# One-tensor divisions on GpSimd, and fixed places for w_out's splits in layer 0 of a two-layer encoder

## The chip, the cores and the metric

One core of a Trainium2 chip runs the whole kernel. The engines named below are TensorE (PE; its weight loads are PEld), VectorE (DVE), ScalarE (ACT), GpSimd (POOL) and SyncE (SP), which issues the DMAs here. The metric is the device time of one execution in microseconds (us), the median of several runs.

## The reference

A two-layer encoder over 1024 tokens of width 1024, all in float32. Layer 0 has three groups of attention heads, layer 1 two; both end with a gate and an output projection:

```python
def even_layer(x, mem_n, table, norm_g, w_in, sink, q_norm, k_norm, w_mem_kv, w_out):
    h = rmsnorm(x, norm_g)
    aq, ak, av, bq, bk, bv, xq, gate = _split(h @ w_in, EVEN_SPLITS)
    y_a = windowed_gqa_sink(heads(aq, A_HEADS), heads(ak, A_KV_HEADS), heads(av, A_KV_HEADS), sink, table)
    ...
    y_b = dense_gqa_blocked(qb, kb, heads(bv, B_KV_HEADS))
    y_x = memory_cross_attention(heads(xq, X_HEADS), mem_n, w_mem_kv)
    y = jnp.concatenate([y_a..., y_b..., y_x...], axis=-1) * jax.nn.silu(gate)
    return x + y @ w_out
```

Group A attends within a window of 128 keys on either side (with a sink logit), group B densely over all 1024 keys, group X over 256 memory tokens. Each of these has a softmax, and so a division by a row's sum. The norms divide by a row's root mean square.

## The kernel before

TensorE multiplies in a reduced float32 form. To keep the accuracy, each operand is split in a high half (the value rounded to that form) and a low half (what is left), and a product is made of three matmuls: high by high, high by low, low by high. The weights are split on the chip as they arrive: for w_in by `load_w` (tiles wr, wh, wl; high on VectorE, L239, low mostly on GpSimd, L241), for w_out by `load_wout` (raw tile wor, halves woh and wol). A w_out piece is 128 rows by 512 columns, and a layer has 16. In layer 0, piece i has its high half on ScalarE (L257) and its low half on GpSimd if i is odd, on VectorE if even (L258).

A piece's raw tile comes from two rings that others use too: "wr" with 2 buffers for even i, "sg" with 3 for odd i. A transfer into a raw buffer waits until the low half of the piece before in it has been made.

Layer 0's attention is a list of steps, which `run_steps` works through. A step of group B (wide: one head, 128 queries, 1024 keys) does this: scores on TensorE (sb), a row minimum on VectorE (L1061), a scalar and the exponential on ScalarE (L1065, L1066; the tile e, and its sum z), the reciprocal rz of the sum on VectorE (L1069) and the division of e by it on GpSimd (L1070). A step of group A (narrow) handles two blocks of 128 queries with at most 384 keys each (L1140, L1144, L1148, and two divisions at L1154). The steps come in the pattern B B A. One step later SP copies the divided tile into another (er) by DMA, which only renames its type. Three steps after its scores the tile is transposed on TensorE (te for B at L540, ta for A at L1175) into a PSUM tile, of which there are two, and split in halves: PTh on ScalarE (L315), PTl on VectorE (L316). Every second step the values are multiplied in (ob at L1083, oa at L1192). The result is joined on ScalarE and VectorE (yt, L437 and L438) and gated on GpSimd (gy, L439).

Between these, projections (acc, L297) are pulled in to fill TensorE, and late in layer 0 parts of the output projection (pre, L662), which need w_out's halves and chunks of the gated result (raw yr, halves yh on ScalarE and yl on VectorE, L318 and L319). `wout_hook` asks for a w_out piece at most once in each of its calls, which come twice in a step.

At the start of the kernel x and the memory tokens are normed: a sum of squares on ScalarE, a power on GpSimd (L229), and a scaling per row, on VectorE (L336) or, with slow=True, on GpSimd (L335). That is so for the fifth x tile and the two memory tiles (memt), which TensorE transposes next (tm, L979).

Every engine works its queue in order. The order of a queue is not the order of the program's text: a scheduler in the framework places the instructions, and `tc.issue_after(x)` holds what is recorded under it behind the instruction x.

Of the kernel before, what the change touches and what calls it, by code (L numbers as in the profile page):

```python
# [14 lines left out]
AF = mybir.ActivationFunctionType  # L15
ALU = mybir.AluOpType
# [139 lines left out]
def encoder_kernel(ctx, tc, A):  # L156
# [93 lines left out]
    def load_wout(l, i, pl):  # L250
        nh, k = divmod(i, 8)
        if k == 0:
            wtile.append([pl.tile([P, 8, 512], F32R, tag="h", name="wo" + c, bufs=4) for c in "hl"])
        raw = sg(M, "wor", F32) if i % 2 else wp.tile([P, 512], F32, tag="wr", name="wor", bufs=2)
        dma(raw, w_out[l][KORD[l][k], :, nh * 512:(nh + 1) * 512])
        hi, lo = (t[:, k, :] for t in wtile[nh])
        (nc.vector.tensor_copy if WHI[l] else nc.scalar.copy)(hi, raw)  # L257
        (nc.gpsimd if i % 2 else nc.vector).tensor_tensor(out=lo, in0=raw, in1=hi, op=ALU.subtract)  # L258
        return hi, lo

    def wout_hook(l, jobs, last, pl):
# [5 lines left out]
                wout[len(wout)] = load_wout(l, len(wout), pl)  # L267

    wout, wtile, half = {}, [], [0]
    chunks = {}  # L270

    def half_done(n=1):
# [59 lines left out]

    def scale_tile(xt, r, slow=False):
        if slow:
            return nc.gpsimd.tensor_tensor(out=xt, in0=xt, in1=r.to_broadcast([P, D]), op=ALU.mult)  # L335
        return nc.vector.tensor_scalar(out=xt, in0=xt, scalar1=r, scalar2=None, op0=ALU.mult)  # L336

    def transpose_tile(xt, hT, t):
# [697 lines left out]
    if True:  # L1036
        def b_step(h, qb):
            st = Step()
            st.sub = qb % 2
            st.fill = 3 if h == 0 else 1  # L1040
            if st.sub == 0:
                bgrp["g"] = {}
            grp = st.grp = bgrp["g"]
            e = [None]

            def s1(h=h, qb=qb, e=e):
                if qb == 2 and h < 5:
                    jobs.ensure("bq%d" % ((h + 1) // 2))
                    load_q(Bq, bq_d, h + 1)
                if h == NB0 and qb == 0:  # L1050
                    jobs.ensure("bq2")
                    open_ab()
                    jobs.ensure("aq0")
                    load_q(Aq, aq_d, 0)
                    a_bias(0)
                Sp = ps_s("sb")
                for j in range(2):
                    qk(Sp[:, j * 512:(j + 1) * 512], Bq[h], qb * P, B["k"][h // 3], B["kl"][h // 3],
                       j * 512, 512)
                mn = stat("mn")  # L1060
                nc.vector.tensor_reduce(out=mn, in_=Sp, op=ALU.min, axis=AX.X)  # L1061
                et = new_e(M)
                z = stat("z")
                mr = stat("mr")
                nc.scalar.activation(mr, mn, AF.Identity, scale=rq[:, qb, h:h + 1])  # L1065
                nc.scalar.activation(et, Sp, AF.Exp, bias=mr, scale=nrq[:, qb, h:h + 1], accum_out=z)  # L1066
                def finish():
                    rz = stat("rz")
                    nc.vector.reciprocal(rz, z)  # L1069
                    nc.gpsimd.tensor_tensor(out=et, in0=et, in1=rz.to_broadcast([P, 1024]), op=ALU.mult)  # L1070
                    e[0] = et
                return finish
            st.s1 = s1
            st.hop = word_copy(M, e)
            st.s2 = dense_s2(M, e, st)
            if st.sub == 1:
                def s3(h=h, qb=qb, grp=grp):
                    ph, pl_ = grp["pt"]
                    acc = ps_a("ob")[:, :256]
                    n = 0  # L1080
                    for kt in range(8):
                        for pt in (ph, pl_):
                            nc.tensor.matmul(acc, B["v"][:, kt, h // 3, :], pt[:, kt, :],  # L1083
                                             start=(n == 0), stop=(n == 15))
                            n += 1
                    y_evac(M, acc, gates[3 + h // 2], h % 2, (qb - 1) * P)
                    if h % 2 == 1 and qb == 7:
                        store_y(0, KORD[0].index(3 + h // 2), gates[3 + h // 2])
                st.s3 = s3
                st.need3 = ("bv", "g%d" % (3 + h // 2))  # L1090
            st.need = ("bk", "bq%d" % (h // 2))
            return st
# [18 lines left out]
    if True:  # L1111
        def a_step(h, p):
# [5 lines left out]
            def s1(h=h, p=p, e=e):  # L1118
# [15 lines left out]
                for j in range(2):  # L1134
# [6 lines left out]
                                                   in1=abias[h][:, c:c + n], scale=1.0,  # L1141
                                                   scalar=nsink[:, h:h + 1], op0=ALU.add, op1=ALU.min,
                                                   accum_out=mn[:, j:j + 1])
                    nc.scalar.activation(et[:, j, c:c + n + 1], et[:, j, c:c + n + 1], AF.Exp,  # L1144
                                         bias=mn[:, j:j + 1], scale=-1.0, accum_out=z[:, j:j + 1])
                def finish():
                    rz = stat("rz2", 2)
                    nc.vector.reciprocal(rz, z)  # L1148
                    for j in range(2):
# [1 line left out]
                        lo, hi = max(0, qb - 1) * P, min(8, qb + 2) * P  # L1151
                        c = lo - (qb - 1) * P
                        ej = et[:, j, c:c + hi - lo]
                        nc.gpsimd.tensor_tensor(out=ej, in0=ej, in1=rz[:, j:j + 1].to_broadcast([P, hi - lo]), op=ALU.mult)  # L1154
                    e[0] = et
                return finish
            st.s1 = s1
# [55 lines left out]
            wout_hook(0, jobs, "g2", r1)  # L1213

    run_steps(steps, jobs, hooks0, lambda i: i % 4 != 3)
    jobs.drain()
    top_stack.close()
    att.close()
# [377 lines left out]
```

## Time and profile before

| | us |
|---|---|
| median of 3 runs | 1242.44 (1242.15 to 1243.17) |
| the profiled execution | 1241.79 |
| its span, first to last instruction | 1240.0 |

| engine | share of the span busy |
|---|---|
| TensorE, matmuls | 97% |
| TensorE, weight loads | 81% |
| VectorE | 65% |
| ScalarE | 53% |
| GpSimd | 33% |

A row of a group reads: line, engine, operation, output<-inputs, output shape<-input shape, count | busy us, mean ns of one | idle us just before them, and what ended most of that. A row of the timeline has start and length in us first, and in square brackets the idle time before it and the instruction that ended it. A row of the waits has: engine, what waits <- what is waited for: us in all, times, the longest. A row of the stretches is explained where it stands.

### The profile page before, as it was taken

The numbers are of one execution on the slowest core, as the hardware profiler recorded it, in microseconds if no ns is written. First come the engines' busy times: TensorE is split into PE (matmuls) and PEld (weight loads), VectorE is DVE, ScalarE is ACT, GpSimd is POOL, SyncE is SP. The second block draws the span as 40 slices with busy tenths as digits, with TensorE's granted clock in tenths as the row PEclk, the third lists the DMA queues.
The fourth block names the chain that finished last, engine by engine and source line by source line (L and its number), as shares of the span: only waits on it lengthen the run. The fifth ranks groups of instructions, "written<-read, shape, count | busy, mean of one in ns | idle before, by whom it ended". The sixth has DMA issues, their size and how long they took to land. (4 is left out here: it accounts for less than half of the span.)

```text
span 1240.0 us, 19680 instructions
## 1 busy us (share of the span) xinstructions
PE 1202.2 (97%) x6806; PEld 999.9 (81%) x6806; DVE 805.7 (65%) x1479; ACT 651.9 (53%) x1453; POOL 412.1 (33%) x390
## 2 busy tenths in 40 slices
PE   5999999999999899999999999999999999999997
PEld 4788888888887788877888788888787878877886
DVE  5547665477777778647356866766767676678544
ACT  6248754367667776533157633544444454456322
POOL 5023365466666655403022221222222121223100
PEclk9999999999999999999999999999999999999999
DMA  6664445545465565376545333242342432546354
GB/s 255 195 194 146 161 170 167 164 159 202 175 229 203 193 236 198 149 211 224 170 151 162 119 111 123 88 143 102 111 134 79 139 112 102 162 141 203 119 197 147
DMA packets 96638, 199.91 MB, mean 161 GB/s; under 512 B 11510, under 2 KB 31222, under 8 KB 96540
## 3 DMA queue, kind: packets, MB, share of 16 engines
q1 hardware_dynamic: 96540, 198.66, 47.7%
q8 instruction: 54, 0.88, 0.3%
q14 instruction: 44, 0.36, 0.1%
HBM read 79.32 MB, written 31.47 MB: 89 GB/s over the span
## 5 line engine op out<-in xcount | busy, mean ns | idle before, releaser
L297 PE MATMUL acc<-h,wh 128*128 128x512 f32 x1536 | 499.2, 398 | 2.1 <-DVE wh L239 0.8
L297 PEld LDWEIGHTS acc<-h,wh 128*128 128x128 f32 x1536 | 283.1, 188 | 66.9 <-issue 12.4
L297 PE MATMUL acc<-h,wl 128*128 128x512 f32 x768 | 304.5, 396 | 1.0 <-POOL wl L241 1.0
L241 POOL TENSOR_TENSOR wl<-wr,wh 128x512 fp32r<-128x512 f32 x96 | 124.4, 1296 | 334.5 <-DVE wh L239 147.2
L316 DVE TENSOR_TENSOR PTl<-te,PTh 128x512 fp32r<-128x512 f32 x224 | 148.3, 686 | 120.9 <-ACT PTh L315 118.3
L1448 ACT ACTIVATE e<-e,mn 128x1024 f32<-128x1024 f32 x96 | 110.1, 1149 | 126.2 <-DVE mn L1445 126.1
L297 PEld LDWEIGHTS acc<-h,wl 128*128 128x128 f32 x768 | 144.5, 188 | 34.0 <-issue 4.7
L315 ACT CAST PTh<-te 128x512 fp32r<-128x512 f32 x224 | 125.0, 590 | 18.3 <-PE te L540 15.2
L1445 DVE CUSTOM_DVE_ANT_0 e<-sc,toep 128x1024 f32<-128x1024 f32 x96 | 114.0, 1216 | 5.8 <-PE sc L1439 5.6
L1070 POOL TENSOR_TENSOR e<-e,rz 128x1024 f32<-128x1024 f32 x48 | 92.5, 1931 | 74.3 <-DVE rz L1069 56.6
L540 PEld LDWEIGHTS te<-identr,er 128*128 128x128 f32 x896 | 92.2, 143 | 18.1 <-issue 3.2
L540 PE MATMUL te<-identr,er 128*128 128x128 f32 x896 | 99.2, 246 | 5.3 <-issue 2.5
L239 DVE CAST wh<-wr 128x512 fp32r<-128x512 f32 x112 | 56.3, 504 | 42.1 <-PE acc L297 17.8
L1457 DVE SCALAR_TENSOR_TENSOR e<-e,mr 128x1024 f32<-128x1024 f32 x48 | 76.3, 1589 | 1.3
L1472 PE MATMUL oc<-PTh,v 128*128 128x256 f32 x384 | 74.8, 288 | 0.3 <-DVE ckl L1341 0.3
L662 PE MATMUL po<-woh,yl 128*128 128x512 f32 (+1 forms) x172 | 65.6, 382 | 0.0
L662 PE MATMUL po<-woh,yh 128*128 128x512 f32 (+1 forms) x172 | 65.6, 381 | 0.0
L662 PE MATMUL po<-wol,yh 128*128 128x512 f32 (+1 forms) x172 | 65.4, 380 | 0.0
L1061 DVE TENSOR_REDUCE mn<-sb 128x1 f32<-128x1024 f32 x48 | 58.4, 1216 | 7.2 <-PE sb L509 6.8
L1472 PEld LDWEIGHTS oc<-PTh,v 128*128 128x128 f32 x384 | 61.4, 191 | 0.6 <-DVE ckl L1341 0.5
L1066 ACT ACTIVATE e<-sb,mr,nrq 128x1024 f32<-128x1024 f32 x48 | 58.0, 1208 | 1.9
L318 ACT ACTIVATE yh<-yr 128x256 fp32r<-128x256 f32 (+2 forms) x56 | 23.9, 447 | 64.1 <-DMA yr<-ysc 30.2
(199 smaller groups left out, 2248.4 us busy)
## 6 DMA issues: line engine op xcount, KB each, us to landing
er<-e SPq DMA_DIRECT2D x112, 512.0 KB, 3.0
wr<-in_w_in SPq DMA_DIRECT2D x96, 256.0 KB, 2.7
ysc<-gy SPq DMA_DIRECT2D x16, 512.0 KB, 2.6
wor<-in_w_out SPq DMA_DIRECT2D x32, 256.0 KB, 3.4
cq<-sg SPq DMA_DIRECT2D x64, 128.0 KB, 2.5
ck<-sg SPq DMA_DIRECT2D x48, 128.0 KB, 2.3
er<-e SPq DMA_DIRECT2D x12, 384.5 KB, 2.9
xpsc<-xh SPq DMA_DIRECT2D x18, 256.0 KB, 2.4
```

Of the source, the lines that this page charges most:

```text
L241: (nc.vector if fast else nc.gpsimd).tensor_tensor(out=lo, in0=raw, in1=hi, op=ALU.subtract)
L297: lastmm[0] = nc.tensor.matmul(acc, a, b[:, k, c0:c0 + n], start=(i == 0), stop=(i == 23))
L315: nc.scalar.copy(hi, src)
L316: return nc.vector.tensor_tensor(out=lo, in0=src, in1=hi, op=ALU.subtract)
L540: nc.tensor.transpose(to[:, i * P:(i + 1) * P], e[0][:, k * P:(k + 1) * P], idt)
L662: lastmm[0] = nc.tensor.matmul(acc, a, b, start=(start and n == 0), stop=(stop and n == 2))
L1061: nc.vector.tensor_reduce(out=mn, in_=Sp, op=ALU.min, axis=AX.X)
L1070: nc.gpsimd.tensor_tensor(out=et, in0=et, in1=rz.to_broadcast([P, 1024]), op=ALU.mult)
L1445: nc.vector.tensor_tensor_reduce(out=et, in0=Sp, in1=toeps[h][:, w0:w0 + 1024], scale=1.0, scalar=BIG, op0=ALU.add, op1=ALU.min, accum_out ...
L1448: nc.scalar.activation(et, et, AF.Exp, bias=mn[:, m:m + 1], scale=-1.0, accum_out=z[:, m:m + 1])
L1457: nc.vector.scalar_tensor_tensor(out=es[0], in0=es[1], scalar=c, in1=es[0], op0=ALU.mult, op1=ALU.add)
L1472: nc.tensor.matmul(acc, V[:, kt, v, :], pt[:, kt, :], start=(n == 0), stop=(n == 23))
```

## The change

Two things change. First, where GpSimd divides a softmax tile (L1070, L1154) or scales a row (L335), it no longer multiplies two tensors, of which one is a column broadcast along the row; it runs the form with one tensor and a factor per partition. Second, in layer 0 the two halves of a w_out piece are held behind the softmax steps: the high half behind the last exponential recorded before it, the low half behind the last division recorded before it, and all low halves are on GpSimd. `behind` keeps those two instructions; after the steps its entry is cleared. Layer 1's pieces are placed as before.

```diff
--- before.py
+++ after.py
@@ -254,8 +254,11 @@
         raw = sg(M, "wor", F32) if i % 2 else wp.tile([P, 512], F32, tag="wr", name="wor", bufs=2)
         dma(raw, w_out[l][KORD[l][k], :, nh * 512:(nh + 1) * 512])
         hi, lo = (t[:, k, :] for t in wtile[nh])
-        (nc.vector.tensor_copy if WHI[l] else nc.scalar.copy)(hi, raw)
-        (nc.gpsimd if i % 2 else nc.vector).tensor_tensor(out=lo, in0=raw, in1=hi, op=ALU.subtract)
+        own = l == 0 and behind["sub"] is not None
+        with (tc.issue_after(behind["exp"].ins) if own else nullcontext()):
+            (nc.vector.tensor_copy if WHI[l] else nc.scalar.copy)(hi, raw)
+        with (tc.issue_after(behind["sub"].ins) if own else nullcontext()):
+            (nc.gpsimd if own or i % 2 else nc.vector).tensor_tensor(out=lo, in0=raw, in1=hi, op=ALU.subtract)
         return hi, lo
 
     def wout_hook(l, jobs, last, pl):
@@ -267,6 +270,7 @@
                 wout[len(wout)] = load_wout(l, len(wout), pl)
 
     wout, wtile, half = {}, [], [0]
+    behind = {"exp": None, "sub": None}
     chunks = {}
 
     def half_done(n=1):
@@ -332,7 +336,7 @@
 
     def scale_tile(xt, r, slow=False):
         if slow:
-            return nc.gpsimd.tensor_tensor(out=xt, in0=xt, in1=r.to_broadcast([P, D]), op=ALU.mult)
+            return nc.gpsimd.tensor_scalar(out=xt, in0=xt, scalar1=r, scalar2=None, op0=ALU.mult)
         return nc.vector.tensor_scalar(out=xt, in0=xt, scalar1=r, scalar2=None, op0=ALU.mult)
 
     def transpose_tile(xt, hT, t):
@@ -1063,11 +1067,12 @@
                 z = stat("z")
                 mr = stat("mr")
                 nc.scalar.activation(mr, mn, AF.Identity, scale=rq[:, qb, h:h + 1])
-                nc.scalar.activation(et, Sp, AF.Exp, bias=mr, scale=nrq[:, qb, h:h + 1], accum_out=z)
+                behind["exp"] = nc.scalar.activation(et, Sp, AF.Exp, bias=mr, scale=nrq[:, qb, h:h + 1], accum_out=z)
                 def finish():
                     rz = stat("rz")
                     nc.vector.reciprocal(rz, z)
-                    nc.gpsimd.tensor_tensor(out=et, in0=et, in1=rz.to_broadcast([P, 1024]), op=ALU.mult)
+                    behind["sub"] = nc.gpsimd.tensor_scalar(out=et, in0=et, scalar1=rz, scalar2=None,
+                                                            op0=ALU.mult)
                     e[0] = et
                 return finish
             st.s1 = s1
@@ -1141,8 +1146,8 @@
                                                    in1=abias[h][:, c:c + n], scale=1.0,
                                                    scalar=nsink[:, h:h + 1], op0=ALU.add, op1=ALU.min,
                                                    accum_out=mn[:, j:j + 1])
-                    nc.scalar.activation(et[:, j, c:c + n + 1], et[:, j, c:c + n + 1], AF.Exp,
-                                         bias=mn[:, j:j + 1], scale=-1.0, accum_out=z[:, j:j + 1])
+                    behind["exp"] = nc.scalar.activation(et[:, j, c:c + n + 1], et[:, j, c:c + n + 1], AF.Exp,
+                                                         bias=mn[:, j:j + 1], scale=-1.0, accum_out=z[:, j:j + 1])
                 def finish():
                     rz = stat("rz2", 2)
                     nc.vector.reciprocal(rz, z)
@@ -1151,7 +1156,8 @@
                         lo, hi = max(0, qb - 1) * P, min(8, qb + 2) * P
                         c = lo - (qb - 1) * P
                         ej = et[:, j, c:c + hi - lo]
-                        nc.gpsimd.tensor_tensor(out=ej, in0=ej, in1=rz[:, j:j + 1].to_broadcast([P, hi - lo]), op=ALU.mult)
+                        behind["sub"] = nc.gpsimd.tensor_scalar(
+                            out=ej, in0=ej, scalar1=rz[:, j:j + 1], scalar2=None, op0=ALU.mult)
                     e[0] = et
                 return finish
             st.s1 = s1
@@ -1213,6 +1219,7 @@
             wout_hook(0, jobs, "g2", r1)
 
     run_steps(steps, jobs, hooks0, lambda i: i % 4 != 3)
+    behind["sub"] = None
     jobs.drain()
     top_stack.close()
     att.close()
```

Line numbers are 4 or 5 higher in the changed program from here on (L1070 is L1074, L1154 is L1159, L257 and L258 are L259 and L261, L315 and L316 are L319 and L320).

The order of the queues is the same in both up to the first w_out piece and again from the end of layer 0's attention. In between it moves. VectorE, where the first pieces are split, before: L1061 is the row minimum of a wide step, L1069 its reciprocal, L438 the join of a result, L316 the low half of a transposed tile.

```order
L316 TENSOR_TENSOR PTa<-ta,PTa 128x2x128
L1061 TENSOR_REDUCE mn<-sb 128x1
L258 TENSOR_TENSOR wol<-wor,woh 128x512 x2
L1069 RECIPROCAL rz<-z 128x1
L438 TENSOR_TENSOR yt<-oa,yt 64x256
L1061 TENSOR_REDUCE mn<-sb 128x1
L316 TENSOR_TENSOR PTl<-te,PTh 128x4x128 x2
```

and now:

```order
L320 TENSOR_TENSOR PTa<-ta,PTa 128x2x128
L1065 TENSOR_REDUCE mn<-sb 128x1
L1073 RECIPROCAL rz<-z 128x1
L442 TENSOR_TENSOR yt<-oa,yt 64x256
L1065 TENSOR_REDUCE mn<-sb 128x1
L320 TENSOR_TENSOR PTl<-te,PTh 128x4x128 x2
```

The two low halves that stood between the minimum and the reciprocal are gone, and no other takes their place. ScalarE at the same place, before: L257 is a high half, L1065 and L1066 the scalar and the exponential of a wide step, L437 the copy for a join, L315 the high half of a transposed tile, L318 that of a chunk of the gated result.

```order
L315 CAST PTa<-ta 128x3x128
L315 CAST PTa<-ta 128x2x128
L257 CAST woh<-wor 128x512 x5
L1065 ACTIVATE mr<-mn,rq 128x1
L1066 ACTIVATE e,z<-sb,mr,nrq 128x1024
L437 COPY yt<-oa 64x256
L315 CAST PTh<-te 128x4x128 x2
L257 CAST woh<-wor 128x512 x2
L1065 ACTIVATE mr<-mn,rq 128x1
```

and now:

```order
L319 CAST PTa<-ta 128x2x128
L1069 ACTIVATE mr<-mn,rq 128x1
L1070 ACTIVATE e,z<-sb,mr,nrq 128x1024
L259 CAST woh<-wor 128x512
L441 COPY yt<-oa 64x256
L319 CAST PTh<-te 128x4x128 x2
L259 CAST woh<-wor 128x512
L1069 ACTIVATE mr<-mn,rq 128x1
L1070 ACTIVATE e,z<-sb,mr,nrq 128x1024
L259 CAST woh<-wor 128x512
```

Five casts of w_out stood in a row ahead of an exponential; now one stands behind each exponential and one behind the halves of the transposed tile. GpSimd, from the first low half on, before: L258 is a low half, L1070 a wide division, L1154 a narrow one, L439 the gating.

```order
L439 TENSOR_TENSOR gy<-yt,gy 64x256
L258 TENSOR_TENSOR wol<-wor,woh 128x512 x3
L1070 TENSOR_TENSOR e<-e,rz 128x1024
L439 TENSOR_TENSOR gy<-yt,gy 64x256
L258 TENSOR_TENSOR wol<-wor,woh 128x512
L1070 TENSOR_TENSOR e<-e,rz 128x1024
L1154 TENSOR_TENSOR e<-e,rz_4672 128x384 x2
L439 TENSOR_TENSOR gy<-yt,gy 64x256 x2
L1070 TENSOR_TENSOR e<-e,rz 128x1024 x2
L258 TENSOR_TENSOR wol<-wor,woh 128x512
```

and now:

```order
L443 TENSOR_TENSOR gy<-yt,gy 64x256
L1074 TENSOR_SCALAR e<-e,rz 128x1024
L261 TENSOR_TENSOR wol<-wor,woh 128x512
L443 TENSOR_TENSOR gy<-yt,gy 64x256
L261 TENSOR_TENSOR wol<-wor,woh 128x512
L1074 TENSOR_SCALAR e<-e,rz 128x1024
L261 TENSOR_TENSOR wol<-wor,woh 128x512 x2
L1159 TENSOR_SCALAR e<-e,rz_4672 128x384
L261 TENSOR_TENSOR wol<-wor,woh 128x512
L1159 TENSOR_SCALAR e<-e,rz_4672 128x384
L443 TENSOR_TENSOR gy<-yt,gy 64x256
L261 TENSOR_TENSOR wol<-wor,woh 128x512
```

The low halves are spread between divisions and gatings, twice as many as before, and the divisions have another form.

## The prediction

> **What bounds the kernel now.** I read the page's busy times first, then the stretches of the span, then who TensorE waits for.
>
> ```profile
> PE 1202.2 (97%) x6806; PEld 999.9 (81%) x6806; DVE 805.7 (65%) x1479; ACT 651.9 (53%) x1453; POOL 412.1 (33%) x390
> ```
>
> TensorE is busy 1202.2 of 1240.0 us. A faster GpSimd or VectorE can therefore give back no more than TensorE's idle time, plus what a lowered clock costs. The stretches say where that lies; their columns are length, busy time (instructions) of PE, PEld, DVE, ACT and POOL, granted clock, DMA share and GB/s:
>
> ```profile
> 0.00:40.00 40.00, 27.56 (x144) 22.43 (x145) 24.79 (x56) 25.98 (x46) 18.37 (x26) 1.00 0.66 227
> 40.00:160.00 120.00, 118.12 (x688) 100.25 (x687) 70.77 (x128) 71.82 (x181) 38.08 (x32) 1.00 0.53 174
> 160.00:380.00 220.00, 219.57 (x1295) 189.26 (x1294) 144.48 (x279) 126.75 (x285) 128.61 (x111) 1.00 0.52 180
> 380.00:440.00 60.00, 52.53 (x306) 44.48 (x306) 46.40 (x83) 43.97 (x99) 37.70 (x33) 0.94 0.63 215
> 440.00:527.00 87.00, 84.94 (x538) 72.45 (x537) 64.63 (x136) 56.46 (x139) 45.28 (x44) 1.00 0.52 191
> 527.00:640.00 113.00, 108.75 (x562) 90.87 (x561) 59.49 (x101) 34.82 (x83) 21.03 (x22) 1.00 0.63 191
> 640.00:1170.00 530.00, 527.46 (x2982) 427.43 (x2981) 366.09 (x645) 274.12 (x578) 117.14 (x116) 1.00 0.38 128
> ```
>
> Layer 0's softmax steps fill 160 to 527 us. From 160 to 380 TensorE idles 220 - 219.57 = 0.43 us: there the divisions on GpSimd, however slow, hold up nothing. From 380 to 440 it idles 60 - 52.53 = 7.47 us, and the clock is at 0.94. That is where w_out of layer 0 is loaded and split. From 440 to 527, with the same softmax steps but no splits, it idles 87 - 84.94 = 2.06 us. TensorE's longest waits between 380 and 527, by releaser:
>
> ```profile
> PE te L540 <- issue: 2.5, 1, 2.5
> PE ob L1083 <- ACT PTh L315: 2.4, 1, 2.4
> PE ob L1083 <- DVE PTl L316: 1.2, 2, 0.6
> PE oa L1192 <- DVE yt L438: 1.1, 1, 1.1
> ```
>
> None of them names GpSimd, so the question is what stands before the instructions waited for. The first one, in order of time (start, length, engine):
>
> ```profile
> 384.74 3.78 POOL L258 TENSOR_TENSOR wol<-wor,woh 128x512 fp32r<-128x512 f32 x3
> 385.11 4.57 DVE L258 TENSOR_TENSOR wol<-wor,woh 128x512 fp32r<-128x512 f32 x2
> 391.12 1.27 DVE L316 TENSOR_TENSOR PTl<-te,PTh 128x512 fp32r<-128x512 f32 x2
> 391.89 0.51 PE L540 MATMUL te<-identr,er 128*128 128x128 f32 x4 [2.48 <-issue]
> ...
> L241 DVE TENSOR_TENSOR wl<-wr,wh 128x512 fp32r<-128x512 f32 x16 | 11.0, 690 | 1.2
> ```
>
> Two low halves on VectorE take 4.57 us; two of the same form elsewhere (the last row: mean 690 ns) take 1.4. They run beside three on GpSimd, which end at 388.52, and end 1.2 us after those: the first of the two seems to have stood until GpSimd was through. Behind them in VectorE's queue is PTl, which frees the PSUM tile that the next transposes need: the first PTl ends near 391.8, TensorE goes on at 391.89. The second wait has another cause:
>
> ```profile
> 422.81 1.24 ACT L257 CAST woh<-wor 128x512 fp32r<-128x512 f32 x2 [1.89 <-DMA wor<-in_w_out]
> 424.15 0.56 ACT L315 CAST PTh<-te 128x512 fp32r<-128x512 f32 x1
> 424.76 0.39 PE L1083 MATMUL ob<-PTh,v 128*128 128x256 f32 x1 [2.36 <-ACT PTh L315]
> ```
>
> ScalarE stood at the high half of a w_out piece whose transfer had not landed, with PTh behind it. The clock, in slices of 3.41 us around the two long waits (same columns):
>
> ```profile
> 388.86:392.27 3.41, 0.93 (x8) 0.58 (x6) 3.41 (x7) 1.36 (x4) 2.44 (x2) 1.00 0.70 222
> 392.27:395.69 3.42, 3.42 (x13) 2.92 (x12) 3.00 (x7) 3.07 (x8) 2.21 (x3) 0.50 0.81 281
> 422.99:426.41 3.42, 1.65 (x11) 1.52 (x12) 1.71 (x6) 3.42 (x9) 1.49 (x2) 1.00 0.18 66
> 429.82:433.23 3.41, 1.86 (x12) 1.49 (x13) 2.65 (x6) 1.74 (x5) 2.69 (x4) 1.00 0.66 266
> 433.23:436.65 3.42, 3.42 (x15) 3.00 (x14) 3.02 (x5) 2.63 (x6) 0.73 (x1) 0.50 0.93 264
> ```
>
> Twice a slice with much idle time is followed by one at half clock. Each costs 3.42 x 0.5 = 1.7 us, together 3.4.
>
> **The change, part by part.** Rows for the prices, four of the whole span, then five of 380 to 440 alone (busy us, mean ns, idle before):
>
> ```profile
> L1070 POOL TENSOR_TENSOR e<-e,rz 128x1024 f32<-128x1024 f32 x48 | 92.5, 1931 | 74.3 <-DVE rz L1069 56.6 <-issue 8.2 <-ACT mr L1065 5.0
> L802 POOL TENSOR_SCALAR nrq<-rq 128x8 f32<-128x8 f32 x6 | 1.5, 252 | 0.5
> L1402 POOL COPY toep<-far 128x768 f32<-128x768 f32 x12 | 10.6, 899 | 35.2 <-DVE mn L1445 34.4 <-ACT h L315 0.7
> L336 DVE TENSOR_SCALAR xt<-xt,r 128x1024 f32<-128x1024 f32 x7 | 5.3, 752 | 3.1 <-POOL r L229 3.1
> ...
> L1070 POOL TENSOR_TENSOR e<-e,rz 128x1024 f32<-128x1024 f32 x7 | 14.4, 2065 | 6.2 <-DVE rz L1069 6.2
> L1066 ACT ACTIVATE e<-sb,mr,nrq 128x1024 f32<-128x1024 f32 x8 | 9.6, 1204 | 0.2
> L258 POOL TENSOR_TENSOR wol<-wor,woh 128x512 fp32r<-128x512 f32 x8 | 10.6, 1341 | 4.0 <-DMA er<-e 2.2 <-ACT woh L257 1.9
> L258 DVE TENSOR_TENSOR wol<-wor,woh 128x512 fp32r<-128x512 f32 x8 | 9.3, 1176 | 0.8 <-ACT woh L257 0.8
> L257 ACT CAST woh<-wor 128x512 fp32r<-128x512 f32 x16 | 9.5, 621 | 7.8 <-DMA wor<-in_w_out 7.8
> ```
>
> *Form of the divisions.* A 1024-wide TENSOR_SCALAR on GpSimd is in no row. Between its 8 elements at 252 ns and the one-operand copy of 768 at 899 ns lies (899 - 252) / 760 = 0.85 ns an element, so 252 + 1016 x 0.85 = 1.1 us. Ends: 0.75 (VectorE's row) and 1.93 (nothing gained). I take 1.1, since the copy runs on the same engine. The 48 wide divisions shed 48 x 0.83 = 40 us of GpSimd's time. From 160 to 380 that is worth 0, at most the 0.43 us of idle time. The Trainium skill ("GPSIMD Engine Reference", section 4.1) calls one-input work on GpSimd "roughly line-rate" and two-input work about half VectorE's speed; at its 1.2 GHz, 1024 elements would be an estimated 0.85 us, which moves no term below by more than 0.1.
>
> *The scalings at the start.*
>
> ```profile
> 26.45 1.90 POOL L335 TENSOR_TENSOR memt<-memt,r 128x1024 f32<-128x1024 f32 x1
> 28.31 0.55 POOL L229 TENSOR_TENSOR r<-v,nhalf 128x1 f32<-128x1 f32 x1
> 28.94 1.90 POOL L335 TENSOR_TENSOR memt<-memt,r 128x1024 f32<-128x1024 f32 x1
> 30.89 0.33 PE L979 MATMUL tm<-ident,memt 128*128 128x128 f32 x1 [1.42 <-POOL memt L335]
> ```
>
> At 1.1 us each the second scaling ends 1.6 us sooner, at 29.2 instead of 30.84, and the wait of 1.42 goes. Some may come back as a later wait for weights: I take -1.2, ends 0 and -1.4. The scaled x tile shortens too, but TensorE stops again near 26 us for x tiles that VectorE scales behind a weight transfer: 0.
>
> *w_out's splits, 380 to 440.* VectorE loses eight low halves, 9.3 of its 46.40 us; GpSimd gains eight at about 1.3, 10.4 us, and sheds 7 x 0.83 in this stretch and some on the narrow ones: 37.70 becomes about 41 of 60. ScalarE's sixteen casts stay, 9.5 us, but stand one or two behind each exponential instead of five and three in a row. What hides the longer GpSimd queue is the distance between a division and its transposes, three steps of 5 us (eight wide exponentials and, by the pattern, four narrow steps make 12 in these 60 us). If it were used up, every 1.3 us of a low half would show. The first wait goes with its cause: PTl would then come after the reduction, and I see at most 0.3 us left. The second and fourth should shrink, because a cast now has its piece asked for a step or two ahead. I leave 2.4 us idle in this stretch: 1.4 at the rate of the stage behind (2.06 x 60 / 87), plus 1.0 for casts that now stand ahead of a PTh. So 7.47 - 2.4 = 5.1 us of waiting, plus 3.4 of clock: -8.5. Ends: -10.9 (everything goes) and -2.5 (two thirds of the idle time and both slow slices stay).
>
> *440 to 527:* the order differs a little, waits are not those of the splits: 0, ends -2.0 and +1.5. *From 527 on* every engine has the same order: 0.
>
> Sum: -1.2 - 8.5 = -9.7 us. The profiled execution took 1241.79 us (span 1240.0 and 1.8 around it), which makes 1232.1; from the median of 1242.44, 0.65 above it, **1232.7 us**.
>
> **Rivals.**
>
> *The fixed places become the wait (slower).* Five raw buffers hold w_out's pieces. From the sixth piece on a transfer waits for a low half, which now always stands behind a division on GpSimd; the transfer then lands late and ScalarE stands at the cast, with PTh behind it.
>
> ```profile
> wor<-in_w_out SPq DMA_DIRECT2D x32, 256.0 KB, 3.4
> ```
>
> The round is a division 1.1, a low half 1.3, its transfer 3.4 and a cast 0.6: 6.4 us, against about 10 for the two steps that a buffer has. For: ScalarE already waited 7.8 us for these transfers, and SP issues in order, so a held w_out transfer holds er behind it. Against: 3.6 us to spare. It decides once a round passes 10 us. Price: eleven pieces in pairs, six waits of the 2.4 us seen above, 14.4, and two more slow slices, 3.4, in place of what is there now (10.9), less 1.2 at the start: +5.7, so 1248. Chance 0.09.
>
> *The splits only look guilty (no change).* Idle time and clock stay because TensorE's new order there meets other waits; only the start gains, 1241.2. For: four different releasers stand in the list. Against: the stage before, with the same steps, idles 0.43 us in 220. Chance 0.11.
>
> *GpSimd's new form is no faster.* The start gives 0; GpSimd has about 48 of 60 us in the splits and still three steps of room: 1234 to 1236. Chance 0.15, inside the forecast's side.
>
> *The clock gives back nothing of its own.* If half clock came for a reason other than these waits, 3.4 us stay: 1236.1. For: the slice at 422.99 held as much idle time, 1.77 us, and no half clock followed. Chance 0.1. The Trainium skill ("TensorE: Matmul & The Clock Gate", the table under "Why this matters for your kernels") warns only of idle gaps over about 3 us; by that rule waits of 2.5 us would cost no clock and the sum would be 1236.1. This trace differs: the clock halves right behind the 2.48 us wait.
>
> **How the numbers follow.** Forecast 0.55, the form no faster 0.15, the clock's own 0.1: together 0.80 for faster by over 0.2%, which is about what a measurement of this kernel can tell from no change. The look of guilt 0.11: within. The fixed places 0.09: slower. The range: its low end is the start at -1.4, 380 to 440 at -10.9 and the stage behind at -2.0, -14.3, so 1228; its high end the poorest of the faster cases with the start at 0, -2.5 and +1.0 behind, 1241.
>
> **What would show it.** Right: in the changed profile the wide divisions on GpSimd near 1.1 us; no low half of w_out on VectorE in layer 0; tm without its 1.4 us wait; from 380 to 440 TensorE idle under 3 us and no slice at 0.50. Wrong: PTh or PTa behind a cast that waits for wor; a division that starts late behind a low half, with te waiting for er; idle time that reappears between 440 and 640, or a slow slice there.

## The result, and the profile after

The changed kernel takes 1255.47 us (median of 4 runs, 1253.47 to 1256.74), the one before 1242.30 (4 runs, 1241.28 to 1243.17): a ratio of 1.0106, 95% interval 1.0094 to 1.0117. It is 13 us slower, where 9.7 us of gain were forecast. The profiled execution took 1253.47 us, its span 1251.7.

The first thing to look at is the operation that the change swapped. The groups of GpSimd by line in the changed kernel, shapes kept apart (columns: line, engine, operation, tiles and shapes, count | busy us, mean ns | idle time before them and what ended it):

```profile
L1074 POOL TENSOR_SCALAR e<-e,rz 128x1024 f32<-128x1024 f32 x48 | 137.1, 2859 | 48.8 <-DVE rz L1073 37.0 <-ACT mr L1069 4.3 <-PE sb L513 3.4
L1159 POOL TENSOR_SCALAR e<-e,rz 128x384 f32<-128x384 f32 x36 | 44.7, 1248 | 3.5 <-issue 2.3 <-POOL e L1074 0.8 <-DVE rz L1153 0.3
L1159 POOL TENSOR_SCALAR e<-e,rz 128x256 f32<-128x256 f32 x12 | 11.2, 937 | 1.6 <-DVE rz L1153 1.4
L339 POOL TENSOR_SCALAR memt<-memt,r 128x1024 f32<-128x1024 f32 x2 | 5.7, 2855 | 0.2
```

A wide division takes 2.86 us; it took 1.93, and 1.1 was assumed. With one tensor less to read it became slower by half. The scalings of memt took 1.90 and take 2.86.

Then where the time went. The stretches below hold the same TensorE instructions as those of the prediction's table (the counts of PE, x144, x688 and so on, are equal), so that the lengths can be compared row by row with 40, 120, 220, 60, 87 and 113 us (same columns):

```profile
0.00:42.94 42.94, 27.80 (x144) 22.54 (x145) 24.87 (x56) 25.95 (x46) 21.23 (x26) 0.96 0.61 211
42.94:162.66 119.72, 118.04 (x688) 100.20 (x687) 70.88 (x128) 71.78 (x181) 38.98 (x31) 1.00 0.54 175
162.66:386.43 223.77, 219.98 (x1295) 189.32 (x1294) 142.58 (x279) 126.66 (x285) 162.37 (x110) 1.00 0.50 175
386.43:451.17 64.74, 53.48 (x306) 44.54 (x306) 39.43 (x76) 44.94 (x102) 56.80 (x41) 0.92 0.57 196
451.17:538.37 87.20, 84.80 (x538) 72.69 (x537) 63.63 (x136) 56.23 (x137) 63.43 (x45) 1.00 0.56 198
538.37:652.34 113.97, 108.97 (x562) 90.78 (x561) 60.12 (x101) 34.99 (x84) 20.99 (x22) 1.00 0.62 189
```

The start is 2.9 us longer (42.94 for 40), the softmax steps ahead of w_out's pieces 3.8 (223.77 for 220), the stage of the pieces 4.7 (64.74 for 60); the rest is within 1 us each. GpSimd's busy time rose from 128.61 to 162.37 us in the second of these and from 37.70 to 56.80 in the third. TensorE's own busy time hardly moved; what grew is its idle time (42.94 - 27.80 = 15.1 us where 12.4 stood, 223.77 - 219.98 = 3.8 where 0.43 stood, 64.74 - 53.48 = 11.3 where 7.5 stood) and, in the fourth row, time at half clock (0.92 where 0.94 stood). The first row has time at half clock too (0.96), but TensorE's busy time there is only 0.24 us longer.

At the start the longer scalings end later, and the transposes of memt wait for them (timeline rows: start, duration, engine, line, operation; in brackets the idle time before it and the releaser):

```profile
27.44 2.86 POOL L339 TENSOR_SCALAR memt<-memt,r 128x1024 f32<-128x1024 f32 x1
30.26 0.57 POOL L229 TENSOR_TENSOR r<-v,nhalf 128x1 f32<-128x1 f32 x1
30.93 2.85 POOL L339 TENSOR_SCALAR memt<-memt,r 128x1024 f32<-128x1024 f32 x1
33.84 0.33 PE L983 MATMUL tm<-ident,memt 128*128 128x128 f32 x1 [2.73 <-POOL memt L339]
```

The wait of 1.42 us that was to go is now 2.73. The scaled x tile costs as much: a low half of w_in stands behind its scaling in GpSimd's queue, and TensorE's wait for that half (wl) rose from 0.6 to 1.9 us. In the softmax steps the delay takes a longer way. Rows of four engines of the changed kernel, in order of time:

```profile
363.56 2.84 POOL L1074 TENSOR_SCALAR e<-e,rz 128x1024 f32<-128x1024 f32 x1
366.43 0.49 SPq L175 DMA_DIRECT2D er<-e  x1
369.68 0.28 ACT L1138 COPY e<-nsink 128x1 f32<-128x1 f32 x2 [2.39 <-DMA er<-e]
373.73 0.39 PE L513 MATMUL sa<-ak,q 128*128 128x256 f32 x1 [1.61 <-DVE mn L1145]
```

Read downwards: the division ends at 366.40, only then can SP ask for the copy of its tile (er), and only when that has landed is the tile e free again. ScalarE stands 2.39 us for it, its exponentials come late, VectorE's score step behind them too, and TensorE stands 1.61 us. Three waits for that score step make the 3.8 us. Before the change the whole stretch held 0.43 us of idle time: "the divisions on GpSimd, however slow, hold up nothing" was true of 1.93 us, not of 2.86.

### The profile page after: what moved, and what is told of

Same layout as the page of the kernel before. It is cut to its first block, busy times and chain, and to the rows that moved or that the text cites. A ratio compares the mean times of both kernels' runs of the same rounds, so it can differ in the third digit from the quotient of the medians.

```text
span 1251.7 us, 19673 instructions
## 1 busy us (share of the span) xinstructions
PE 1203.6 (96%) x6806; PEld 1000.3 (80%) x6806; DVE 796.3 (64%) x1471; ACT 652.4 (52%) x1453; POOL 486.6 (39%) x398
## 5 line engine op out<-in xcount | busy, mean ns | idle before, releaser
L320 DVE TENSOR_TENSOR PTl<-te,PTh 128x512 fp32r<-128x512 f32 x224 | 148.3, 686 | 119.3 <-ACT PTh L319 116.9
L1074 POOL TENSOR_SCALAR e<-e,rz 128x1024 f32<-128x1024 f32 x48 | 137.1, 2859 | 48.8 <-DVE rz L1073 37.0
L319 ACT CAST PTh<-te 128x512 fp32r<-128x512 f32 x224 | 124.9, 591 | 15.5 <-PE te L544 14.3
L229 POOL TENSOR_TENSOR r<-v,nhalf 128x1 f32<-128x1 f32 (+1 forms) x28 | 19.2, 689 | 117.4 <-DVE v L1298 96.5
L1065 DVE TENSOR_REDUCE mn<-sb 128x1 f32<-128x1024 f32 x48 | 58.4, 1217 | 7.1 <-PE sb L513 6.6
L1512 POOL TENSOR_TENSOR gy<-O,gy 128x256 f32<-128x256 f32 x24 | 18.6, 775 | 112.6 <-DVE O L1509 112.5
```

The source lines that it names most:

```text
L319: nc.scalar.copy(hi, src)
L320: return nc.vector.tensor_tensor(out=lo, in0=src, in1=hi, op=ALU.subtract)
L1074: behind["sub"] = nc.gpsimd.tensor_scalar(out=et, in0=et, scalar1=rz, scalar2=None, op0=ALU.mult)
```

## The experiments

**Which half of the change costs the time.** Four kernels: the changed one with its divisions and scalings put back to two tensors (e1); the kernel before with the one-tensor form and nothing else (e2); the kernel before with the one-tensor form in the three scalings of the start alone (e3); the first of these without the fixed places (e4).

```diff
e1, against the changed kernel
-  behind["sub"] = nc.gpsimd.tensor_scalar(out=et, in0=et, scalar1=rz, scalar2=None, op0=ALU.mult)
+  behind["sub"] = nc.gpsimd.tensor_tensor(out=et, in0=et, in1=rz.to_broadcast([P, 1024]), op=ALU.mult)
...
e2, against the changed kernel
-  own = l == 0 and behind["sub"] is not None
+  own = False
e3, against the kernel before
-  return nc.gpsimd.tensor_tensor(out=xt, in0=xt, in1=r.to_broadcast([P, D]), op=ALU.mult)
+  return nc.gpsimd.tensor_scalar(out=xt, in0=xt, scalar1=r, scalar2=None, op0=ALU.mult)
e4, against e1
-  with (tc.issue_after(behind["exp"].ins) if own else nullcontext()):
+  with nullcontext():
-  with (tc.issue_after(behind["sub"].ins) if own else nullcontext()):
+  with nullcontext():
```

> The fixed places and the sixteen low halves on GpSimd stay; divisions and scalings go back to the two-tensor form. Theory A (the one-tensor form is the whole loss: 2.86 us against 1.93 for 1024 elements, 1.25 against 0.83 for 384, so that GpSimd ends late): the start loses its 2.95 us of delay and the stage of w_out's splits is no worse than before, 1234 to 1242 us. Theory B (the fixed places cost on their own, as the slower rival of the prediction has it: casts or low halves waiting in line): about 6 us of the delay between 380 and 480 stay, 1246 to 1250 us.

> The kernel before with the one-tensor form in all divisions and scalings, and nothing else. Theory A: start +2.95, the attention before w_out's pieces +1.7 to +3.5, and in the 60 us behind them GpSimd is still overfull (37.7 us, plus 7 x 0.93 and 12 x 0.4, with eight low halves): 1248 to 1257 us. Theory B: only the parts of the delay ahead of the splits, 1245 to 1248 us.

> The kernel before with the one-tensor form in the three scalings of the start alone. Both theories: two scalings of memt at 2.86 instead of 1.90 push tm back by 1.9 us, and if TensorE's idle time there again falls into one slice at half clock, 1.0 to 1.7 more: 1244 to 1246 us; under 1243 if the delay at the start of the changed kernel came from something else.

> As the first of these four (two-tensor form, sixteen low halves on GpSimd), without the fixed places: casts and low halves stand where the scheduler puts them. If the places are worth something, 1 to 8 us above that one; if only the engine of the low halves matters, within 1 us of it; below it if the places themselves cost.

Measured: e1 1241.26 us, ratio 0.9992 (0.9983 to 1.0002); e2 1256.71, 1.0112 (1.0097 to 1.0127); e3 1245.19, 1.0025 (1.0013 to 1.0036); e4 1243.43, 1.0009 (1.0000 to 1.0018). Theory A holds, theory B falls: the one-tensor form alone costs 1.1%, as much as the whole change, and the start alone 0.25%. The splits' half costs nothing; in e1 it gains at most 0.2%. The places are worth about the 2 us by which e4 lies above e1, though the two intervals just touch.

But e1 leaves a second question. Its divisions take 1.9 us as before, its splits stand where the change puts them, and 8.5 us should have gone from the stage of the pieces. The row of that stage in e1:

```profile
380.00:440.00 60.00, 52.81 (x303) 44.20 (x301) 37.22 (x74) 43.41 (x99) 44.81 (x40) 0.91 0.58 201
```

TensorE idles 60 - 52.81 = 7.19 us there (7.47 before), and the clock is at 0.91 (0.94). The groups of ScalarE in the same stretch of e1, and the chain that leads to the longest wait:

```profile
L259 ACT CAST woh<-wor 128x512 fp32r<-128x512 f32 x16 | 9.8, 618 | 2.0 <-DMA wor<-in_w_out 2.0
L322 ACT ACTIVATE yh<-yr 128x512 fp32r<-128x512 f32 x4 | 2.5, 632 | 6.4 <-DMA yr<-ysc 6.4
...
396.76 1.29 POOL L261 TENSOR_TENSOR wol<-wor,woh 128x512 fp32r<-128x512 f32 x1
398.08 0.38 SPq L175 DMA_DIRECT2D yr<-ysc  x1
402.66 0.63 ACT L322 ACTIVATE yh<-yr 128x512 fp32r<-128x512 f32 x1 [4.54 <-DMA yr<-ysc]
404.52 0.51 PE L513 MATMUL sa<-ak,q 128*128 128x384 f32 x1 [2.63 <-ACT e L1070]
```

ScalarE's wait for pieces fell from 7.8 us to 2.0, as hoped. In its place it waits 6.4 us for y's rows (yr, split for the first output products), where it waited 2.0 before. The loads of yr use the two raw buffers of tag `wr`, and the even pieces of w_out lie in the same two; SP asked for the first yr at 389.70 before, and here at 398.08, 0.03 us behind a low half on GpSimd. An exponential stands behind that yh, and TensorE behind the exponential. That is 2.63 of TensorE's 7.19 us there; the rest is in shorter waits.

**Whether that pair of buffers is the cause.** Three variants of e1: even low halves back on VectorE, at their fixed places (e5); all pieces in the three buffers that yr does not use (e10); the wide divisions among the pieces on VectorE (e7).

```diff
e5
-  (nc.gpsimd if own or i % 2 else nc.vector).tensor_tensor(out=lo, in0=raw, in1=hi, op=ALU.subtract)
+  (nc.gpsimd if i % 2 else nc.vector).tensor_tensor(out=lo, in0=raw, in1=hi, op=ALU.subtract)
e10
-  raw = sg(M, "wor", F32) if i % 2 else wp.tile([P, 512], F32, tag="wr", name="wor", bufs=2)
+  raw = sg(M, "wor", F32) if i % 2 or l == 0 else wp.tile([P, 512], F32, tag="wr", name="wor", bufs=2)
e7
+  if 0 < len(wout) < 16:
+      behind["sub"] = nc.vector.tensor_scalar(out=et, in0=et, scalar1=rz, scalar2=None, op0=ALU.mult)
+  else:
       behind["sub"] = nc.gpsimd.tensor_tensor(out=et, in0=et, in1=rz.to_broadcast([P, 1024]), op=ALU.mult)
```

> As the two-tensor form with fixed places (first of the runs before), but the low halves of the even pieces go back to VectorE, each at its place behind a division. The even pieces lie in the two raw buffers that the loads of y (yr) use too. Theory C: in that run yr came only at 398.1 us (before: 389.7) since a GpSimd low half had to free this pair; freed by VectorE in 0.7 us, the 4.5 us wait of ScalarE for yr goes, and with it 2.6 us of TensorE's idle time and perhaps a half-clock slice: 1235 to 1240 us. Theory D (SP's issue in order is what holds yr, whoever frees the pair; or VectorE's low halves stand ahead of PTl as before): 1240 to 1244 us.

> As the two-tensor form with fixed places, but all sixteen pieces of layer 0 lie in the other three raw buffers, so that yr never waits for a low half. Theory C: ScalarE's wait for yr goes as above, but pieces come later with three buffers instead of five, so that casts wait for them: 1236 to 1243 us, with the wait for yr under 1.5 us in the trace. Theory D: yr still lands after 400 us, as it stands behind pieces in SP's queue: 1241 to 1248 us.

> As the two-tensor form with fixed places, but the wide divisions that fall among w_out's pieces are done by VectorE as one-tensor scalings (0.75 us by the row of its own scalings, against 1.9 on GpSimd). If GpSimd's queue is what is left of the loss, it sheds about 7 x 1.9 = 13 of its 44.8 us in 60 and TensorE's 7.2 us of idle time there fall under 4, with fewer half-clock slices: 1233 to 1239 us. If it is the buffers or SP's queue: 1240 to 1243 us.

Measured: e5 1242.31 us, ratio 0.9999 (0.9989 to 1.0010); e10 1246.99, 1.0031 (1.0017 to 1.0044); e7 1237.82, 0.9964 (0.9954 to 0.9975).

e10 did what theory C says in the trace and not in the time: ScalarE no longer waits for yr at all, and, as theory C has it, longer for pieces (4.0 us where e1 has 2.0). But:

```profile
389.24 1.27 DVE L320 TENSOR_TENSOR PTl<-te,PTh 128x512 fp32r<-128x512 f32 x2
391.51 5.53 DVE L323 SCALAR_TENSOR_TENSOR yl<-yr,yh 128x512 fp32r<-128x512 f32 x1
...
390.90 1.29 POOL L261 TENSOR_TENSOR wol<-wor,woh 128x512 fp32r<-128x512 f32 x1
392.16 1.89 POOL L1074 TENSOR_TENSOR e<-e,rz 128x1024 f32<-128x1024 f32 x1
394.01 2.48 POOL L261 TENSOR_TENSOR wol<-wor,woh 128x512 fp32r<-128x512 f32 x2
...
397.69 0.58 PE L1087 MATMUL ob<-PTl,v 128*128 128x256 f32 x1 [4.37 <-DVE PTl L320]
```

With yr there early, its low half yl (VectorE, 0.69 us elsewhere) falls beside a run of GpSimd's two-tensor work without a gap, and takes 5.53 us: it ends 0.55 us after that run. PTl stands behind it, and TensorE 4.37 us. It is the kind of stall that opens the stage in the kernel before, where two low halves on VectorE took 4.57 us beside three on GpSimd. So the wait has at least three forms, and an edit that removes one of them meets the next: for a piece, for yr, for VectorE. Theory C's price did not come in e5 either, by another way: yr was asked for even later, at 401.26, yet ScalarE waits only 0.6 us for it (6.4 in e1), and TensorE still idles 60 - 52.97 = 7.0 us, 2.6 of them in one wait for VectorE's join and 2.0 in waits for PTl. That is inside theory D's range and fits its second reason. e7, which takes the wide divisions away from GpSimd, is the first that gains:

```profile
380.00:440.00 60.00, 55.36 (x338) 46.91 (x338) 46.78 (x94) 47.25 (x110) 38.00 (x37) 0.97 0.66 225
```

TensorE idles 4.6 us there in place of e1's 7.2 (under 4 was expected). That fits the thought that long runs on GpSimd lie behind all three forms, but it does not show it. e5 took as much off GpSimd (38.12 us busy, e7 38.00, e1 44.81) and gained nothing; e7 also keeps the low halves off VectorE and makes the division itself shorter (0.89 us).

**When one tensor is slower than two.** Two kernels that differ from the one before in the three scalings of the start alone, each scaling in another form. They leave out two scalings (e9) and one (e14), so only the durations count; as wholes they took 1243.27 and 1242.40 us, one execution each.

```diff
e9:  x tile, first memt, second memt
+  nc.gpsimd.tensor_scalar(out=xt, in0=xt, scalar1=1.0, scalar2=None, op0=ALU.mult)
+  nc.gpsimd.tensor_copy(out=xt, in_=xt)
+  nc.gpsimd.tensor_scalar(out=xt, in0=xt, scalar1=r, scalar2=0.0, op0=ALU.mult, op1=ALU.add)
e14: x tile, first memt, second memt
+  nc.gpsimd.tensor_scalar(out=xt, in0=xt, scalar1=r, scalar2=1.0, op0=ALU.mult, op1=ALU.mult)
+  nc.gpsimd.tensor_scalar(out=xt, in0=xt, scalar1=0.0, scalar2=None, op0=ALU.add)
+  nc.gpsimd.tensor_scalar(out=xt, in0=xt, scalar1=0.0, scalar2=r, op0=ALU.add, op1=ALU.mult)
```

> A look at single durations on GpSimd. The kernel before, with the three scalings at the start changed: the x tile by an immediate 1.0 (its scaling is left out), the first memt tile by a copy onto itself (its scaling is left out), the second memt tile by its factor per partition and a second operation that adds 0. If the factor per partition makes the form slow, the immediate runs near 1.2 us; if the operation does, all one-tensor arithmetic is near 2.86 us and the copy near 1.2; if even a copy of 1024 in place is near 2.8, the width or the place is what counts. A second operation costs nothing or up to another 1.3 us.

> A second look at single durations on GpSimd, in the three scalings at the start of the kernel before: the x tile by its factor and then by 1.0 (two multiplications), the first memt tile by a single addition of 0.0 (its scaling is left out), the second memt tile by an addition of 0.0 and then its factor. If it is the single operation that is slow, whatever it is: 1.1, 2.8, 1.1 us. If it is the multiplication alone, and an addition in any place makes it fast: 2.8, 1.1, 1.1 us.

GpSimd's groups from 0 to 60 us, of e9 (three rows) and of e14 (three rows):

```profile
L338 POOL TENSOR_SCALAR xt<-xt 128x1024 f32<-128x1024 f32 x1 | 2.8, 2790 | 0.0
L341 POOL TENSOR_SCALAR memt<-memt,r 128x1024 f32<-128x1024 f32 x1 | 1.1, 1140 | 0.1
L340 POOL COPY memt<-memt 128x1024 f32<-128x1024 f32 x1 | 1.0, 1042 | 0.0
```

```profile
L340 POOL TENSOR_SCALAR memt<-memt 128x1024 f32<-128x1024 f32 x1 | 2.8, 2806 | 0.0
L338 POOL TENSOR_SCALAR xt<-xt,r 128x1024 f32<-128x1024 f32 x1 | 1.1, 1132 | 0.1
L341 POOL TENSOR_SCALAR memt<-memt,r 128x1024 f32<-128x1024 f32 x1 | 1.1, 1124 | 0.1
```

It is neither the factor per partition nor the multiplication. With a single operation the form takes 2.8 us (a multiplication by an immediate or by a factor, an addition of an immediate); with a second operation, in the three pairs tried, 1.13. A second operation that changes nothing makes it 2.5 times as fast.

**The change with that second operation.** The changed kernel with an addition of 0.0 in each division and scaling (e11); the same without fixed places and with the splits of before (e12); the same with even low halves on VectorE, at their places (e13).

```diff
e11, at all three places
-  behind["sub"] = nc.gpsimd.tensor_scalar(out=et, in0=et, scalar1=rz, scalar2=None, op0=ALU.mult)
+  behind["sub"] = nc.gpsimd.tensor_scalar(out=et, in0=et, scalar1=rz, scalar2=0.0, op0=ALU.mult, op1=ALU.add)
e12, beside it
-  own = l == 0 and behind["sub"] is not None
+  own = False
e13, beside e11's edit
-  (nc.gpsimd if own or i % 2 else nc.vector).tensor_tensor(out=lo, in0=raw, in1=hi, op=ALU.subtract)
+  (nc.gpsimd if i % 2 else nc.vector).tensor_tensor(out=lo, in0=raw, in1=hi, op=ALU.subtract)
```

> The changed kernel with a second operation (add 0.0) in its divisions and scalings, everything else as it is. The look at single durations gave 1.14 us for this form and 2.79 for the one with a single operation, at 1024 elements. Theory E (the single operation is the whole loss): wide divisions near 1.1 us here too, and the kernel falls from 1255 to below the one before. How far then tests the rest of the prediction with the duration that it assumed: 1232.7 us if the waits of w_out's stage go as forecast; 1236 to 1240 us if pieces, the loads of y and VectorE's own waits keep most of the 7 us of idle time that the two-tensor form had there. Theory F (1.14 us holds at the start only, the divisions stay near 1.9 or 2.8 beside other traffic): 1241 to 1256 us.

> The kernel before with the two-operation form in all divisions and scalings, w_out's splits as before. Theory E: the start gains the 1.2 us forecast for it, and w_out's stage keeps the VectorE low halves that hold up PTl: 1238 to 1242 us. If the places in the changed kernel are worth their forecast 8.5 us, this one is 6 to 8 us above the first of these three; if most of the gain is GpSimd's shorter queue, within 2 us of it.

> As the first of these three, with the low halves of even pieces on VectorE at their fixed places. VectorE's operations on two SBUF operands were seen to last until a run of GpSimd's two-tensor work ends (5.5 us for one that takes 0.7 alone). If that is the cause of the rest, this one is 2 to 5 us above the first; if the engine of the even halves does not matter, within 1 us of it.

Measured: e11 1235.42 us, ratio 0.9948 (0.9933 to 0.9964); e12 1236.79, 0.9955 (0.9943 to 0.9968); e13 1232.75, 0.9923 (0.9911 to 0.9936). Theory E holds, and e11 and e12 come out about 1 us below what was expected of either. e12 lies 1.4 us above e11: of the two outcomes named for it, the one in which most of the gain is GpSimd's shorter queue, and not the 6 to 8 us of the places. GpSimd's divisions in e11, and its stage of the pieces and the stage behind:

```profile
L1074 POOL TENSOR_SCALAR e<-e,rz 128x1024 f32<-128x1024 f32 x48 | 54.5, 1136 | 91.7 <-DVE rz L1073 70.2 <-issue 12.9 <-ACT mr L1069 5.1
L1159 POOL TENSOR_SCALAR e<-e,rz 128x384 f32<-128x384 f32 x36 | 20.9, 587 | 18.3 <-issue 11.4 <-DVE rz L1153 5.6 <-POOL e L1074 0.8
L1159 POOL TENSOR_SCALAR e<-e,rz 128x256 f32<-128x256 f32 x12 | 5.8, 481 | 7.1 <-DVE rz L1153 4.0 <-issue 3.0
...
380.00:440.00 60.00, 53.21 (x323) 44.04 (x322) 39.49 (x82) 45.19 (x105) 41.41 (x42) 1.00 0.66 224
440.00:527.00 87.00, 86.06 (x534) 73.81 (x533) 60.84 (x128) 53.80 (x129) 30.66 (x40) 1.00 0.56 203
```

From 1255 to 1235 us by one more operand in each division and scaling. TensorE still idles 6.8 us from 380 to 440, but no slice there is at half clock, and behind 440 it idles 0.9 us in place of 2.06. Of ScalarE's waits in the stage, those for yr, the longest in e1, are now the second longest:

```profile
L259 ACT CAST woh<-wor 128x512 fp32r<-128x512 f32 x16 | 9.9, 618 | 1.5 <-DMA wor<-in_w_out 1.5
L322 ACT ACTIVATE yh<-yr 128x512 fp32r<-128x512 f32 x4 | 2.5, 632 | 4.7 <-DMA yr<-ysc 4.7
```

e13 was expected above e11 and lies 2.7 us below it: with divisions this short, the even low halves are better on VectorE. With the two-tensor form they were not (e5 1242.31, e1 1241.26). The runs of e13 and e11 do not overlap (1232.21 to 1234.15 and 1234.24 to 1239.54), but the two profiled executions took 1234.15 and 1234.24, so that the traces cannot show where the 2.7 us lie. What they show: VectorE's eight low halves in that stage cost 0.91 us on average, where they cost 1.26 in e5 at the same places and 1.18 before, and GpSimd has eight fewer (the last row is its busy time, 32.38 for e11's 41.41):

```profile
L261 DVE TENSOR_TENSOR wol<-wor,woh 128x512 fp32r<-128x512 f32 x8 | 7.3, 913 | 1.4 <-ACT woh L259 1.3
...
380.00:440.00 60.00, 55.28 (x324) 45.55 (x323) 47.33 (x87) 44.41 (x103) 32.38 (x34) 0.97 0.67 228
```

The runs side by side, as ratios to the kernel before:

| splits of w_out | two tensors | one tensor, one operation | one tensor, two operations |
|---|---|---|---|
| as before | 1 | 1.0112 (e2) | 0.9955 (e12) |
| all on GpSimd, placed (the change) | 0.9992 (e1) | 1.0106 (the change) | 0.9948 (e11) |
| alternating, placed | 0.9999 (e5) | not run | 0.9923 (e13) |

Down the first two rows the change's splits give 0.06 to 0.08% in each form, about 1 us, which no interval tells from nothing; across the columns the form decides. e13 beats both kernels, by 0.8% and 1.8%.

## Why the prediction was wrong

- **Form of the divisions** (1.1 us, ends 0.75 and 1.93): this step failed, and with it the sign. 2.86 us was measured. Two faults lie in it. The 1.1 was drawn as a line between two different operations, eight elements of a TENSOR_SCALAR and 768 of a COPY. The eight-wide row is nearly all fixed cost: with 2.5 ns an element, (2859 - 937) / 768 from the rows of 1024 and 256, its 252 ns would hold 20 ns that tell of the rate. And the range had no end above "nothing gained", though no row of the trace excluded a loss. That a second operation gives 1.13 us, the value assumed, is chance.
- **The start** (-1.2): with the assumed duration it gains more than the end of -1.4. In e11 TensorE no longer waits for memt, the second memt tile's first transpose stands at 28.9 us instead of 30.89, and the same 144 TensorE instructions fit in 37.99 us (first row below; the second is the stage of the pieces). The x tile's scaling, priced at 0, seems part of that: the pair of powers behind it starts at 24.50 us instead of 25.00. With 2.86 us the start lost 2.9 us in the changed kernel.

```profile
0.00:37.99 37.99, 26.83 (x144) 21.46 (x145) 23.96 (x56) 25.81 (x46) 16.06 (x26) 1.00 0.69 239
377.12:434.30 57.18, 50.39 (x306) 41.54 (x306) 37.80 (x76) 44.39 (x101) 39.10 (x40) 1.00 0.61 210
```

- **160 to 380, nothing**: argued from 0.43 us of idle time with divisions "however slow". Idle time of zero only says that the present duration fits. At 2.86 us it cost 3.8 us.
- **w_out's splits** (-8.5): the second step that failed. With the form taken out of the comparison they give about 1 us (e1). The two causes named were real, and both went (ScalarE's wait for pieces from 7.8 to 2.0 us, the stall of VectorE's low halves), but the 7.5 us of idle time stayed at 7.2, the longest wait behind yr. I counted SP's and the buffers' effect on w_out's own pieces and overlooked that yr shares two of the five buffers. Even with divisions of 1.1 us the stage keeps 6.8 us of idle time (e11); over the same 306 TensorE instructions it takes 57.18 us for 60, 2.8 of the 8.5 us forecast, and 1.1 us more go behind 440.
- **The rivals**: "the form no faster" was priced at 1234 to 1236; e1 is that case and takes 1241.3, by the same 8.5 us that did not come. "The fixed places become the wait" had the right kind of mechanism, a buffer freed only behind a division on GpSimd, but at the wrong transfer, and not as a loss. "The splits only look guilty" named e1's outcome (idle time and clock stay, 1241.2); that the figure fits is luck, for its 1.2 us come from the start, which e1 leaves as it was. No rival said that the new form is slower than the old, and that was the result. (The range's high end, 1241, takes +1.0 for the stage behind where the part-by-part list has +1.5; with that it is 1241.4, which changes nothing here.)
- **The clock**: in e11 no slice between 380 and 440 is at half clock, though 6.8 us of idle time are left there, the longest wait 1.5 us; in e13, with a wait of 1.9, one half-clock slice remains. So the rival in which the clock gives nothing back falls for e11. But the link between waits and clock is looser than the prediction has it. Its second half-clock slice follows the slice at 429.82, not the one of the long wait, 422.99. And the start of e7 is at half clock from 20.0 to 23.4 us behind waits of 0.96 and 0.57 us; the kernel before has 0.82 and 0.57 at that place, and full clock. The two rows, before first:

```profile
20.00:23.41 3.41, 3.41 (x18) 2.65 (x17) 2.80 (x8) 2.08 (x5) 2.58 (x3) 1.00 0.99 382
20.00:23.41 3.41, 3.41 (x11) 2.58 (x11) 2.80 (x7) 2.10 (x4) 2.62 (x3) 0.51 1.01 383
```

That slice cost e7 no time: its first 40 us hold the same 144 TensorE instructions as before. The price of 1.7 us for each holds only where no other wait takes it up.

How the last 6.8 us divide between SP's order, the shared buffers and VectorE's stalls was not separated: each edit that took one away brought out another.

## What to carry to other kernels

Take the rate of an operation from a row of the same operation at the same width, or measure it alone before it goes into 96 places; and leave the range open to a loss when no such row exists. When a wait is removed, list everything that shares its buffers and its queue, for that is where the time will be found again. An idle time of nothing on a bound engine is no proof of slack on another.

## What the hardware showed that was not expected

A one-tensor operation on GpSimd (128 x 1024, f32) takes 2.79 to 2.86 us with one operation and 1.12 to 1.14 with two; the copy takes 1.04, the two-tensor form 1.90. Why, no run here shows. One thing narrows it. Beside both forms VectorE's yl, of the same shape and begun 0.24 or 0.25 us behind the start of a division, took 1.15 us (0.42 in e2, begun 1.17 us behind such a start) and ended 1.39 or 1.40 us after that start (changed kernel, then e11):

```profile
477.21 2.85 POOL L1074 TENSOR_SCALAR e<-e,rz 128x1024 f32<-128x1024 f32 x1 [0.81 <-ACT yh L322]
477.45 1.15 DVE L323 SCALAR_TENSOR_TENSOR yl<-yr,yh 128x256 fp32r<-128x256 f32 x1
...
458.29 1.13 POOL L1074 TENSOR_SCALAR e<-e,rz 128x1024 f32<-128x1024 f32 x1 [1.58 <-DVE rz L1073]
458.54 1.15 DVE L323 SCALAR_TENSOR_TENSOR yl<-yr,yh 128x256 fp32r<-128x256 f32 x1
```

What the slow form adds, 1.7 us, held up GpSimd's own queue and what waits for it, and not VectorE.

VectorE's work on two SBUF operands stood still beside GpSimd's two-tensor work: 5.53 us for 0.69 in e10, until a run of four GpSimd instructions ended, while two PTl, which read PSUM, took 1.27 us, 0.63 each, beside a GpSimd low half just before. It is not always the whole run. Later in e10 yl was through 0.55 us after the first of two instructions, and the second, a division that takes 1.89 us elsewhere, took 2.34:

```profile
410.98 1.29 POOL L261 TENSOR_TENSOR wol<-wor,woh 128x512 fp32r<-128x512 f32 x1
412.24 2.34 POOL L1074 TENSOR_TENSOR e<-e,rz 128x1024 f32<-128x1024 f32 x1
411.38 1.45 DVE L323 SCALAR_TENSOR_TENSOR yl<-yr,yh 128x512 fp32r<-128x512 f32 x1
```

What decides between the two cases, no run here shows. The Trainium skill ("SBUF — State Buffer", section "SBUF: two separate sides") calls the port pair of the two engines an exclusive lock, held for one instruction. The trace agrees that it is no sharing; it adds that VectorE can miss its turn between GpSimd instructions that follow each other without a gap, and it differs beside the slow form, where yl was through 1.46 us before the division's end.
